# Hybrid encoder trunk on one core: rotary reads, output-weight loads, the MLP norm's mean and the half-piece mixes put in other places

## The chip, the cores and the metric

The kernel runs on one core of a Trainium2 chip. The metric is the device time of one execution in microseconds (us), the median of several runs; lower is better. Engines are named as the profile names them: PE (matrix products), DVE, ACT, POOL, SP (which only issues transfers here).

## The reference, cut to what matters

One sequence of 1024 tokens of width 1024 goes through two layers, all in float32. Layer 0 mixes tokens by grouped-query attention (16 heads of 64, 4 key heads), layer 1 by a chunked gMLP unit; each is followed by a squared-ReLU MLP of hidden width 4096. Every sub-layer is normed and modulated by a conditioning vector.

```python
q = apply_rope(rmsnorm(q, q_g), cos, sin)        # q and k of the attention
o = softmax(q @ k.T * HEAD_DIM ** -0.5) @ v ;  x += gate * (o @ w_o)
h = modulate(rmsnorm(x, g), shift, scale)        # before each mixer and each MLP
u, v = split(gelu(h @ w_in + b_in))              # gMLP
v = einsum('gpq,bnqgc->bnpgc', w_s, layernorm(v)) + b_s
x += gate * ((u * v) @ w_out)
x += gate * (square(relu(h @ w_in)) @ w_out)     # MLP
```

There are 16 position-mixing matrices of 128x128, each for a group of 192 of the 3072 gMLP channels.

## The kernel before, in words

Each large product is made in two levels. A float32 operand is split into a high and a low half (ACT copies the high half, a CAST; DVE or POOL subtracts for the low half), and three matmuls per pair of tiles take the place of one: lines L575 to L577 for q, k and v, L469 to L471 for the input products of gMLP and MLP, L1212 to L1214 for their output products. The input products are also cut into blocks that are combined by sums and differences (the "forms", t tiles), so that seven block products take the place of eight; `forms_b` builds the forms of the second half of the blocks from the normed x while PE already works on the first. The sub-layers follow each other: qkv, attention, the output weights wo, MLP 0, gMLP, MLP 1. A scheduler orders the instructions of each engine from the order of the program; on an engine, an instruction that waits holds up all behind it.

The places that the change and the prediction touch:

- qkv, about 100 to 130 us. `qk_sums` (L623) squares each q tile on ACT (L622) and sums it per head on DVE; `qk_rstd` adds the mean and takes the root (L641, L245 to L250); `qk_rope` applies the rotary tables: DVE multiplies the PSUM tile (L633, and L635 twice), POOL adds (L636); `qk_scale` (L649, POOL) multiplies by the root. For four q tiles (`ps`, named qkv_145 and qkv_146 in the order) squares, sums and roots come first, the rotary reads of PSUM behind them. The PSUM tiles are then taken by the next products (L575). `kstacks` (L681, PE transposes into PSUM tiles kt) needs tiles that DVE's L611 (`values`, low halves of v) has read.
- the end of attention, 455 to 505 us. The wo slabs come through `issue_w`: a transfer (L113, 512 KB), a CAST on ACT (L116), a subtraction on POOL (L117). Slots w (4 of them) are shared with the slabs that POOL scales for the conditioning (L199, L200). The x tiles (`load_x`, L520) are issued by SP ahead of the first two wo slabs. ACT also does what attention waits for: the exponentials (L957), the copies of PSUM tiles (L937, L968, L994, L996).
- the norm of each MLP. `norm_ss` sums squares on PE (L274), takes mean and epsilon on DVE (L276), a power on POOL (L242) and four scaled copies of the identity on ACT (L284); `norm_rb` broadcasts by a product (rb, L289), and `forms_b` starts with L334 on DVE. HB and HR count in which units of the input product the two calls stand.
- the mixes of the gMLP, 1507 to 1772 us. For each of 24 channel tiles of 128 and both halves of the tokens `mix` makes a product per 128 tokens (L1661) and DVE adds the bias (L1665); a channel tile with ct % 3 == 1 straddles two groups, so that its mix has two pieces of 64 channels: 8 tiles, 16 mixes of 16 matmul records with 64 columns of weights. The mixes stand between the products L469 to L471, spread by `at`.

Of the kernel before, what the change touches and what calls it, by code (L numbers as in the profile page):

```python
# [13 lines left out]
AF = mybir.ActivationFunctionType  # L14
ALU = mybir.AluOpType
# [4 lines left out]
D = 1024  # L20
# [16 lines left out]
def encoder_kernel(ctx: ExitStack, tc: tile.TileContext, t: dict, out: bass.AP):  # L37
# [18 lines left out]
    def hold(ins):  # L56
        if pinned[0]:
            pin(ins)
# [22 lines left out]
    def wide(tag, dt=F32, shape=(1024,)):  # L81
        if tag == "c":
            return cwide(dt, shape)
        return mem.tile([P] + list(shape), dt, tag=tag, name=nm(tag), bufs=SLOTS[tag])
# [17 lines left out]
    kw = (KT, P)  # L102
    plan = [(("wo", m), kw) for m in (*range(KT), *range(WA))]

    issued = []

    def issue_w():
        key, shape = plan[len(issued)]
        raw = wide("w", F32, shape)
        src = t[key[0]]  # L110
        for i in key[1:]:
            src = src[i]
        nc.sync.dma_start(raw, src)  # L113
        hi = wide("s", F32R, shape)
        lo = wide("s", F32R, shape)
        S.copy(hi, raw)  # L116
        G.tensor_tensor(lo, raw, f32(hi), ALU.subtract)  # L117
        issued.append((key, hi, lo))
# [148 lines left out]
    def norm_rstd(sqs, bank):  # L267
        return norm_rb(norm_ss(sqs, bank), bank)

    def norm_ss(sqs, bank, wide_dg=False):  # L270
        acc = sqs.acc
        ps = bank("ss")[:, :4]
        for j in range(4):
            hold(T.matmul(ps[:, j : j + 1], acc[:, j * P : (j + 1) * P], ones[:, 0:1], start=True, stop=True))  # L274
        ms = small.tile([P, 4], F32, tag="ms", name=nm("ms"))
        hold(V.tensor_scalar(ms, ps, 1.0 / D, EPS, ALU.mult, ALU.add))  # L276
        r = rsqrt_small(ms, 4)
        dg = slot()
        if wide_dg:
            hold(V.tensor_tensor(dg.rearrange("p (j q) -> p j q", j=4), ident.unsqueeze(1).broadcast_to([P, 4, P]),  # L280
                                 r.unsqueeze(2).broadcast_to([P, 4, P]), ALU.mult))
            return dg
        for j in range(4):
            S.activation(dg[:, j * P : (j + 1) * P], ident, AF.Copy, scale=r[:, j : j + 1])  # L284
        return dg
# [257 lines left out]
    if True:  # L543
# [100 lines left out]
        def q_sums(src):  # L644
            return qk_rstd(qk_sums(src))
# [177 lines left out]

        pk = banks(False)
        qkv_mm(0, 0, pk, hs1)
        rr2 = q_sums(ps)
        q_rope(0, 2, ps, rr2, (0, 1), G)
        qkv_mm(0, 1, pk, hs1)
        q_rope(0, 2, ps, rr2, (2, 3), G)
        qkv_mm(0, 2, pk, hs1)  # L830
        qkv_w(2, 0, V, True)
        kk = k_split(kd)
# [83 lines left out]
    with ExitStack() as es:  # L916
# [132 lines left out]
        for i in range(nu + 2):  # L1049
            u0 = units[i] if i < nu else None  # L1050
            u1 = units[i - 1] if 0 < i <= nu else None
            u2 = units[i - 2] if i > 1 else None
            if u0:
                if i % 4 == 0:
                    qst, nxt = nxt, []
                u0.qst = qst
            for op in ORDER.split():
                f, w, j = op[0], int(op[1]), int(op[2])
                if f == "m":
                    if i in deferred:  # L1060
                        deferred.pop(i)()
                    elif i == WO_AT - 6:
                        load_sel()
                    elif WO_AT <= i < WO_AT + 10:
                        if i == WO_AT:
                            copy_sel()
                        elif i == WO_AT + 1:
                            wo_sums(0)
                        else:
                            wo_prep(0, i - WO_AT - 2)  # L1070
                    elif i >= nu:
                        mods(1)
                    if late_mods and i % 4 == 1:
                        late_mods.pop()()
                    if i % 4 == 3 and 12 <= i < 52:
                        late_mods.append(mod_ahead())
                    slabs.step(bank_x, i >= 14 and (i % 4 in (1, 2) or i % 8 == 3))
                elif f == "q":
                    if i % 4 == 0 and w == 0 and i + 4 < nu:
                        qh = q_stage(units[i + 4].qq, units[i + 4].g)  # L1080
                    if i % 4 > 1 and w == 1 and i + 2 < nu:
                        q_trans(qh, i % 4 - 2, nxt)
                else:
                    u = (u0, u1, u2)[w]
                    if u and (i or f not in "se"):
                        stages[f](u, j)
            if i == nu - 1:
                x[0] = [load_x(0, k) for k in range(KT)]
            if i == nu:
                wo_mm(0, (0,), bank_x)  # L1090
# [249 lines left out]
    def mlp(layer, fs, sqs, done, hook):  # L1340
        hidden = forms_dram(16)
        out_ = Out(t["wm"][layer], hidden, 4, mod[:, layer, 5])
        quad = {}
        f = {}
        stores = []

        def sink(c, m, hf):
            S.activation(c, c, AF.Relu)
            S.activation(c, c, AF.Square)
            p = m // 2  # L1350
            quad[(m, hf)] = c
            q = early((m % 2, hf))
            if q:
                nc.scalar.dma_start(hidden[p][q], c)
                if q == "1" and p < FIRST:
                    del quad[(m, hf)]
                elif q == "2" and p < FIRST:
                    quad[(m - 1, 0)] = slot()
                    nc.sync.dma_start(quad[(m - 1, 0)], hidden[p]["1"])
            else:  # L1360
                tiles = {(j, h): quad.pop((m + j, h)) for j in range(2) for h in range(2)}
                stores.extend(spread(tiles, hidden[p], slot, V))

        n = 16 * 7
        rest = []
        halves = None if layer else Halves(late)

        def at(i):
            more(f, RW, None)
            if halves:  # L1370
                h = i - 13
                if 0 <= h < 2 * KT:
                    spill(h // KT, (h % KT,))
                elif h == 2 * KT:
                    halves.start()
                elif h == 2 * KT + 4:
                    halves.silu()
                    halves.load()
                    halves.load()
                elif h > 2 * KT + 6 and h % MX == 0:  # L1380
                    halves.step()
            if i == HB[layer]:
                rest.append(norm_ss(sqs[0], bank_y))
            elif i == HB[layer] + HR[layer]:
                rest[:] = forms_b(f, x[1], layer, 1, norm_rb(rest[0], bank_y, True), "5473")
            elif i > HB[layer] + HR[layer] and rest:
                rest.pop(0)()
            if stores and i % 7 > 0 and i % 7 != 6:
                stores.pop(0)()
            out_.ahead(i - n)  # L1390

        yield from winograd(lambda m: t["wi"][layer, m], 16, f, sink, FIRST, at, lambda: (cut(8), f.update(fs[0])))

        def at_out(i):
            if stores and i > 2:
                stores.pop(0)()
            if i == CUT:
                cut(4)
            if halves and i in XL:
                load_xs(*XL[i])  # L1400
            if hook and i >= out_.n - out_.tail:
                hook(i - out_.n + out_.tail)

        if halves:
            load_xs(*XL[-1])
        out_.run(at_out, done)
# [203 lines left out]
    def gmlp(f, sqB, done, hook):  # L1610
        rest = []

        def at(i):
            more(f, RW, None)
            if i == HBV:
                spill(0)
                rest.append(norm_ss(sqB, bank_y))
            elif i == HBV + 2:
                rest[:] = forms_b(f, x[1], 1, 0, norm_rb(rest[0], bank_y), "5734", True)
            elif rest and i in (*range(HBV + 3, HBV + 7), 10, 12, 16, 20):  # L1620
                rest.pop(0)()
                if len(rest) == 4:
                    spill(1)
# [65 lines left out]
        for p in range(12):  # L1689
            i = 7 * p  # L1690
            at(i - 4 if p else -1, load_v, p)
            for j in range(8):
                at(i - 1 + (j // 4) if p else -1, norm_v, p, j)
            if p % 3 == 0:
                at(i - 5 if p else -1, consts_load, p // 3)
                at(i if p else 3, consts, p // 3)
            for k, (j, hf) in enumerate(order):
                at(i + 2 + k + (0 if p else 2), mix, 2 * p + j, hf)
                at(i + ((3, 6, 6, 7)[k] if p else (6, 6, 7, 8)[k]), times, p, j, hf)
            at(i + (8 if p else 9), spread_uv, p)  # L1700
        steps.sort(key=lambda e: e[:2])

# [68 lines left out]
HK = 3  # L1771
LK = 4
HB = (2, 1)
HR = (2, 1)
HBV = 1
PRE = 2
WO_AT = 53
# [73 lines left out]
```

## Time and profile before

| | us |
|---|---|
| median of 3 runs (2625.09 to 2626.88) | 2625.38 |
| the profiled execution | 2627.54 |
| its span | 2625.8 |
| PE busy in it | 2601.6 (99%) |
| DVE busy | 2183.1 (83%) |
| ACT busy | 1451.1 (55%) |
| POOL busy | 723.2 (28%) |

The profiled execution took 2.2 us more than the median, and 1.7 us of it lie outside its span. A row of the timeline gives start, duration, engine, line of the program, operation, tiles and, in brackets, how long the engine had been idle before it and what released it. A matmul's duration is longer than its share of PE, since the next starts before it ends; PE's pace is read from starts.

### The profile page before, as it was taken

To read this page: it belongs to the slowest core of one execution; us is meant where nothing else is said; L and a number is where in the kernel's file an instruction comes from. 1 tells how busy PE (TensorE), PEld (TensorE's weight loads), DVE (VectorE), ACT (ScalarE), POOL (GpSimd) and SP (SyncE) were. 2 spreads that over 40 slices of the span, in tenths; PEclk is the share of its full clock that TensorE was granted. 3 is DMA by queue.
4 is the path that set the end of the run, shared out by engine and by line. 5 is a ranking of instruction groups with operands and counts; after the bars stand their busy time and mean duration, and the time that the engine had idled before them with its cause. 6 is when DMAs were issued, how large, how long until landed. Compare 5 with 4: busy or idle time off the path is not lost. (4 is left out here: it accounts for less than half of the span.)

```text
span 2625.8 us, 37307 instructions
## 1 busy us (share of the span) xinstructions
PE 2601.6 (99%) x12860; PEld 2172.2 (83%) x12860; DVE 2183.1 (83%) x3276; ACT 1451.1 (55%) x2612; POOL 723.2 (28%) x531
## 2 busy tenths in 40 slices
PE   9999999999999999999999999999999999999999
PEld 7789999888788888888888888888888788888887
DVE  7868999887989989877897687788979977789974
ACT  4569999854654455446543354445456645465442
POOL 0238776533000004430122054451520000005400
PEclk9999999999999999999999999999999999999999
DMA  8010222234486788545243355568641554487461
GB/s 306 27 33 9 74 88 75 97 112 145 168 288 245 270 310 306 192 133 172 82 136 121 120 174 175 178 204 305 237 141 50 177 179 156 153 310 268 149 211 58
DMA packets 208752, 435.39 MB, mean 166 GB/s; under 512 B 23025, under 2 KB 35441, under 8 KB 208562
## 3 DMA queue, kind: packets, MB, share of 16 engines
q1 hardware_dynamic: 181682, 395.24, 44.7%
q10 hardware_dynamic: 26880, 37.76, 4.0%
q8 instruction: 102, 1.67, 0.3%
q14 instruction: 88, 0.72, 0.1%
HBM read 310.23 MB, written 122.68 MB: 165 GB/s over the span
## 5 line engine op out<-in xcount | busy, mean ns | idle before, releaser
L1212 PE MATMUL out<-t,s 128*128 128x512 f32 x1232 | 479.9, 390 | 0.9 <-ACT t L328 0.8
L1213 PE MATMUL out<-t,s 128*128 128x512 f32 x1232 | 479.3, 389 | 0.7 <-DVE t L329 0.7
L1214 PE MATMUL out<-t,s 128*128 128x512 f32 x1232 | 478.9, 389 | 0.0
L469 PE MATMUL w<-t,s 128*128 128x512 f32 x1168 | 459.8, 395 | 0.9 <-ACT t L328 0.5
L470 PE MATMUL w<-t,s 128*128 128x512 f32 x1168 | 455.2, 390 | 1.8 <-DVE t L329 1.8
L471 PE MATMUL w<-t,s 128*128 128x512 f32 x1168 | 454.7, 389 | 0.0
L329 DVE TENSOR_TENSOR t<-t,t 128x512 fp32r<-128x512 f32 x408 | 324.7, 806 | 36.2 <-ACT t L328 29.0
L328 ACT CAST t<-t 128x512 fp32r<-128x512 f32 x408 | 245.3, 617 | 122.2 <-DMA t<-hf 71.7
L1213 PEld LDWEIGHTS out<-t,s 128*128 128x128 f32 x1232 | 231.2, 188 | 50.2 <-DVE t L329 1.8
L1212 PEld LDWEIGHTS out<-t,s 128*128 128x128 f32 x1232 | 231.2, 188 | 50.2 <-ACT t L328 1.7
L1214 PEld LDWEIGHTS out<-t,s 128*128 128x128 f32 x1232 | 231.2, 188 | 48.1
L454 ACT CAST s<-w 128x512 fp32r<-128x512 f32 x292 | 173.4, 616 | 161.4 <-PE w L471 104.3
L470 PEld LDWEIGHTS w<-t,s 128*128 128x128 f32 x1168 | 219.3, 188 | 49.7 <-DVE t L329 5.2
L469 PEld LDWEIGHTS w<-t,s 128*128 128x128 f32 x1168 | 219.3, 188 | 49.4 <-issue 2.9
L471 PEld LDWEIGHTS w<-t,s 128*128 128x128 f32 x1168 | 219.2, 188 | 45.6
L455 DVE TENSOR_TENSOR s<-w,s 128x512 fp32r<-128x512 f32 x292 | 221.8, 766 | 41.1 <-ACT s L454 40.6
L1194 ACT CAST s<-t 128x512 fp32r<-128x512 f32 x240 | 148.2, 620 | 187.0 <-PE out L1214 136.3
L1180 POOL TENSOR_TENSOR w<-w,t 128x512 f32<-128x512 f32 x20 | 34.2, 1721 | 767.7 <-DMA t<-hf 691.5
L1195 DVE TENSOR_TENSOR s<-t,s 128x512 fp32r<-128x512 f32 x240 | 195.1, 814 | 56.1 <-ACT s L1194 55.4
L951 DVE TENSOR_REDUCE mx<-s 128x1 f32<-128x1024 f32 x128 | 156.2, 1220 | 30.5 <-PE s L948 29.2
L974 DVE TENSOR_TENSOR t<-t,t 128x512 fp32r<-128x512 f32 x256 | 164.1, 681 | 17.1 <-ACT t L968 16.4
L984 PE MATMUL o<-t,t 128*128 128x256 f32 x1024 | 162.6, 291 | 0.0
(251 smaller groups left out, 5089.1 us busy)
## 6 DMA issues: line engine op xcount, KB each, us to landing
t<-hf SPq DMA_DIRECT2D x320, 256.0 KB, 4.0
hf<-c SPq DMA_DIRECT2D x156, 256.0 KB, 3.4
w<-in_wi_dram SPq DMA_DIRECT2D x64, 512.0 KB, 4.5
hf<-c ACTq DMA_DIRECT2D x96, 256.0 KB, 2.7
w<-in_ada_dram SPq DMA_DIRECT2D x36, 512.0 KB, 3.9
x<-in_ada_dram SPq DMA_DIRECT2D x64, 256.0 KB, 5.4
t<-in_wm_dram SPq DMA_DIRECT2D x64, 256.0 KB, 4.7
wf<-w SPq DMA_DIRECT2D x64, 256.0 KB, 3.0
```

The lines of the kernel that those rows point to most:

```text
L328: S.copy(hi, src)
L329: (eng or V).tensor_tensor(lo, src, f32(hi), ALU.subtract)
L454: S.copy(hi, src)
L455: V.tensor_tensor(lo, src, f32(hi), ALU.subtract)
L469: T.matmul(ps, hi[:, a], th, start=kt == 0, stop=False)
L470: T.matmul(ps, hi[:, a], tl, start=False, stop=False)
L471: T.matmul(ps, lo[:, a], th, start=False, stop=kt == 3)
L974: pin(V.tensor_tensor(lo, pt, f32(hi), ALU.subtract))
L1195: V.tensor_tensor(lo, src, f32(hi), ALU.subtract)
L1212: T.matmul(ps, hi[:, a], th, start=begin and kt == 0, stop=False, **g)
L1213: T.matmul(ps, hi[:, a], tl, start=False, stop=False, **g)
L1214: T.matmul(ps, lo[:, a], th, start=False, stop=end and kt == 3, **g)
```

## The change

1. In qkv the four rotary steps of that q set stand as `qk_rope`, two ahead of the sums of squares and two behind; the roots and the scalings are taken later.
2. `issue_w` is parted: `fetch_w` issues a slab's transfer, and two of them stand ahead of the x loads in attention's last unit.
3. `norm_ss` takes mean and epsilon by an ACTIVATE on ACT in both MLPs and in the gMLP's norm; in MLP 0 the broadcast product stands one unit earlier (HR 2 to 1); in both MLPs `forms_b` takes the differences for its forms "5" and "4" later (apart).
4. The two mixes of a straddling channel tile stand in the same unit, next to each other.

```diff
+    def fetch_w():
+        key, shape = plan[len(fetched)]
         raw = wide("w", F32, shape)
...
         nc.sync.dma_start(raw, src)
+        fetched.append(raw)
+
+    def issue_w():
+        key, shape = plan[len(issued)]
+        if len(fetched) == len(issued):
+            fetch_w()
+        raw = fetched[len(issued)]
...
+        if act:
+            S.activation(ms, ps, AF.Identity, scale=1.0 / D, bias=epst)
+        else:
+            hold(V.tensor_scalar(ms, ps, 1.0 / D, EPS, ALU.mult, ALU.add))
...
-        rr2 = q_sums(ps)
-        q_rope(0, 2, ps, rr2, (0, 1), G)
+        ds = [qk_rope(ps[j], 0, j, 1, V, G) for j in range(2)]
+        sums2 = qk_sums(ps)
+        ds += [qk_rope(ps[j], 0, j, 1, V, G) for j in range(2, 4)]
         qkv_mm(0, 1, pk, hs1)
-        q_rope(0, 2, ps, rr2, (2, 3), G)
+        rr2 = qk_rstd(sums2)
+        for j in range(4):
+            qk_scale(ds[j], rr2, j)
+            qn[(j, 1)] = ds[j]
...
             if i == nu - 1:
+                fetch_w()
+                fetch_w()
                 x[0] = [load_x(0, k) for k in range(KT)]
...
-                rest.append(norm_ss(sqs[0], bank_y))
+                rest.append(norm_ss(sqs[0], bank_y, act=True))
             elif i == HB[layer] + HR[layer]:
-                rest[:] = forms_b(f, x[1], layer, 1, norm_rb(rest[0], bank_y, True), "5473")
+                rest[:] = forms_b(f, x[1], layer, 1, norm_rb(rest[0], bank_y, True), "5473", True)
...
-                at(i + 2 + k + (0 if p else 2), mix, 2 * p + j, hf)
+                at(i + (4 if j in two else next(free)) + (0 if p else 2), mix, 2 * p + j, hf)
...
-HR = (2, 1)
+HR = (1, 1)
```

DVE in qkv. Tile qkv_145 holds the first two q tiles, qkv_146 the other two; qss are the sums, y, e and r the root. Before, the last reads of qkv_145 stand here:

```order
L633 TENSOR_TENSOR t_227_967<-qkv_145_658,t_141_638 128x512
L250 SCALAR_TENSOR_TENSOR r_212_909<-e_214_913,y_213_910 128x32
L641 TENSOR_SCALAR qss_219_945<-qss_219_945 128x32
L635 TENSOR_TENSOR t_228_968<-qkv_145_658,t_142_640 128x8x32
L246 RECIPROCAL y_225_960<-y_225_960 128x32
L635 TENSOR_TENSOR t_228_968<-qkv_145_658,t_142_640 128x8x32
L248 SCALAR_TENSOR_TENSOR e_226_963<-y_225_960 128x32
L633 TENSOR_TENSOR t_229_974<-qkv_145_658,t_141_638 128x512
L249 TENSOR_TENSOR e_226_963<-e_226_963,qss_219_945 128x32
L635 TENSOR_TENSOR t_230_975<-qkv_145_658,t_142_640 128x8x32
```

In the change they begin sixteen rows earlier, at the place of the first root:

```order
L652 TENSOR_SCALAR qss_201_865<-qss_201_865 128x16
L644 TENSOR_TENSOR t_219_945<-qkv_145_658,t_141_638 128x512
L254 RECIPROCAL y_205_874<-y_205_874 128x16
L646 TENSOR_TENSOR t_220_946<-qkv_145_658,t_142_640 128x8x32
L256 SCALAR_TENSOR_TENSOR e_206_877<-y_205_874 128x16
L646 TENSOR_TENSOR t_220_946<-qkv_145_658,t_142_640 128x8x32
L257 TENSOR_TENSOR e_206_877<-e_206_877,qss_201_865 128x16
L644 TENSOR_TENSOR t_221_951<-qkv_145_658,t_141_638 128x512
L258 SCALAR_TENSOR_TENSOR r_204_873<-e_206_877,y_205_874 128x16
```

L644, L646 and L652 are L633, L635 and L641 of before. Further on, one cast's low half (L577, L566 of before) that stood ahead of the reads for `kstacks` now stands behind them.

ACT at the end of attention. s are high halves of weight slabs, w the slabs. Before, the first wo slab's CAST stands in a late unit, between copies L968:

```order
L968 CAST t_1643_6318<-t_1642_6313 128x512
L116 CAST s_1841_7023<-w_1840_7021 128x1024
L968 CAST t_1646_6331<-t_1645_6326 128x512
L957 ACTIVATE c_1647_6333,rowsum_87<-s_1639_6304,mx_1640_6309 128x1024
L994 COPY t_1277_4968<-o_1632_6281 64x256
L996 COPY t_1649_6346<-o_1632_6281 64x256
L896 CAST t_1653_6358<-t_442_1903 128x512
L116 CAST s_1844_7029<-w_1843_7027 128x1024
```

In the change (lines L124, L983, L952, L972, L1009, L1011 are L116, L968, L937, L957, L994, L996 of before) both stand some six units earlier:

```order
L1011 COPY t_1510_5826<-o_1491_5754 64x256
L124 CAST s_1842_7025<-w_1817_6943 128x1024
L983 CAST t_1515_5848<-t_1514_5843 128x512
L952 CAST t_1517_5855<-qt_1516_5850 128x512
L983 CAST t_1520_5864<-t_1519_5859 128x512
L972 ACTIVATE c_1521_5866,rowsum_87<-s_1511_5831,mx_1512_5836 128x1024
L983 CAST t_1526_5882<-t_1525_5877 128x512
L983 CAST t_1529_5895<-t_1528_5890 128x512
L972 ACTIVATE c_1530_5897,rowsum_87<-s_1522_5868,mx_1523_5873 128x1024
L1009 COPY t_1140_4466<-o_1513_5838 64x256
L1011 COPY t_1532_5910<-o_1513_5838 64x256
L124 CAST s_1844_7029<-w_1818_6945 128x1024
```

The CAST stands right ahead of the copies of the unit in which the x loads are issued. On SP the order is now: first wo slab, two x tiles, second wo slab, six x tiles.

PE among the mixes (w and t are the products between them, x the operands of a mix). Before, the two mixes of the straddling tile 1 stand forty products apart, the first so:

```order
L471 MATMUL w6_3763_16191<-t_3361_13980,s_3753_16109 128x512
L1661 MATMUL mix_3764_16205<-x_3678_15717,x_3740_16046 64x128 x4
L1661 MATMUL mix_3764_16205<-x_3678_15717,x_3741_16048 64x128 x4
L469 MATMUL w5_3771_16228<-t_3367_14049,s_3755_16136 128x512
L470 MATMUL w5_3771_16228<-t_3368_14050,s_3755_16136 128x512
```

In the change (L1678 is L1661, L480 to L482 are L469 to L471):

```order
L482 MATMUL w4_3780_16258<-t_3425_14328,s_3758_16160 128x512
L1678 MATMUL mix_3781_16272<-x_3678_15717,x_3740_16046 64x128 x4
L1678 MATMUL mix_3781_16272<-x_3678_15717,x_3741_16048 64x128 x4
L1678 MATMUL mix_3783_16283<-x_3678_15717,x_3742_16050 64x128 x4
L1678 MATMUL mix_3783_16283<-x_3678_15717,x_3743_16052 64x128 x4
L480 MATMUL w7_3786_16298<-t_3385_14118,s_3762_16187 128x512
```

All eight pairs stand so, with nothing between them.

## Rows read from the trace of the kernel before

**Rows 1.** What PE waited for: releaser, total us, times, longest us.

```profile
PE w L470 <- DVE t L329: 1.8, 6, 0.5
PE w L469 <- ACT t L328: 1.7, 2, 1.2
```

**Rows 2.** PE in qkv, timeline 111 to 127 us.

```profile
113.59 0.47 PE L575 MATMUL qkv<-t,t 128*128 128x512 f32 x1 [2.11 <-DVE t L635]
...
115.05 0.60 PE L575 MATMUL qkv<-t,t 128*128 128x512 f32 x1
...
118.44 0.42 PE L576 MATMUL qkv<-t,t 128*128 128x512 f32 x1
...
126.31 0.89 PE L681 MATMUL kt<-identr,t 128*128 128x128 f32 x8
```

**Rows 3.** Stretches: us, busy PE, PEld, DVE, ACT, POOL, granted clock, DMA share, GB/s.

```profile
116.00:118.00 2.00, 2.00 (x6) 1.53 (x5) 2.00 (x2) 0.00 (x0) 2.00 (x2) 0.50 0.00 0
500.80:504.20 3.40, 3.40 (x14) 2.91 (x13) 1.39 (x3) 3.39 (x7) 3.40 (x7) 0.50 0.46 119
2044.40:2050.00 5.60, 5.17 (x22) 3.96 (x23) 5.60 (x11) 4.09 (x8) 0.00 (x0) 1.00 0.52 187
```

**Rows 4.** DVE in qkv, timeline 99 to 127 us.

```profile
103.35 0.25 DVE L246 RECIPROCAL y<-y 128x16 f32<-128x16 f32 x1 [1.60 <-ACT y L245]
...
117.14 1.76 DVE L566 TENSOR_TENSOR s<-c,s 128x512 fp32r<-128x512 f32 x1
...
124.04 0.68 DVE L672 TENSOR_TENSOR t<-t,t 128x512 fp32r<-128x512 f32 x1
...
125.84 1.41 DVE L611 TENSOR_TENSOR t<-qkv,t 128x256 fp32r<-128x256 f32 x4
```

**Rows 5.** ACT in qkv, timeline 105 to 113 us.

```profile
108.79 0.62 ACT L560 CAST w<-c 128x512 fp32r<-128x512 f32 x1 [1.24 <-PE qkv L577]
```

**Rows 6.** ACT at the end of attention, timelines 456 to 470 and 492 to 503 us.

```profile
460.46 0.37 ACT L996 COPY t<-o 64x256 f32<-64x256 f32 x1
...
461.35 0.59 ACT L937 CAST t<-qt 128x512 fp32r<-128x512 f32 x1
...
497.85 1.05 ACT L116 CAST s<-w 128x1024 fp32r<-128x1024 f32 x1 [2.27 <-DMA w<-in_wo_dram]
```

**Rows 7.** The same place on PE.

```profile
462.30 0.60 PE L965 MATMUL t<-ident,c 128*128 128x128 f32 x4
...
500.55 1.59 PE L965 MATMUL t<-ident,c 128*128 128x128 f32 x7 [1.89 <-ACT c L957]
```

**Rows 8.** POOL at 458 us, and the landing times of the wo slabs (L113, 14 of them).

```profile
458.36 2.40 POOL L200 TENSOR_TENSOR s<-s,w 128x1024 f32<-128x1024 f32 x1
...
DMA to landing us min/median/max: 3.2/3.7/8.8
```

**Rows 9.** The norm of MLP 0: ACT, DVE, POOL and PE, timelines 650 to 661 us.

```profile
653.57 0.59 ACT L474 COPY c<-w 128x512 f32<-128x512 f32 x1
656.79 1.28 ACT L284 ACTIVATE t<-ident,r 128x128 f32<-128x128 f32 x4 [2.62 <-POOL r L242]
...
658.61 0.69 DVE L329 TENSOR_TENSOR t<-t,t 128x512 fp32r<-128x512 f32 x1 [2.94 <-ACT t L328]
...
655.75 1.01 POOL L242 TENSOR_TENSOR r<-ms,mhalf 128x4 f32<-128x4 f32 x1 [19.06 <-DVE ms L276]
...
655.07 0.39 PE L469 MATMUL w<-t,t 128*128 128x512 f32 x1
```

**Rows 10.** PE around a straddling mix and around a whole one, timelines 1625 to 1632 us.

```profile
1629.62 0.39 PE L471 MATMUL w<-t,s 128*128 128x512 f32 x1
...
1631.30 0.40 PE L470 MATMUL w<-t,s 128*128 128x512 f32 x1
...
1625.99 0.39 PE L471 MATMUL w<-t,s 128*128 128x512 f32 x1
...
1627.34 0.40 PE L470 MATMUL w<-t,s 128*128 128x512 f32 x1
```

More of the change, by code (lines that the diff above doesn't have):

```diff
@@ L103, in encoder_kernel @@
     plan = [(("wo", m), kw) for m in (*range(KT), *range(WA))]
-    issued = []
-    def issue_w():
-        key, shape = plan[len(issued)]
+    issued, fetched = [], []
+    def fetch_w():
+        key, shape = plan[len(fetched)]
         raw = wide("w", F32, shape)
@@ L113, in issue_w @@
         nc.sync.dma_start(raw, src)
+        fetched.append(raw)
[4 more added lines that the diff above has]
+        raw = fetched[len(issued)]
+        fetched[len(issued)] = None
         hi = wide("s", F32R, shape)
@@ L268, in norm_rstd, with norm_ss @@
         return norm_rb(norm_ss(sqs, bank), bank)
-    def norm_ss(sqs, bank, wide_dg=False):
+    def norm_ss(sqs, bank, wide_dg=False, act=False):
         acc = sqs.acc
@@ L275, in norm_ss @@
         ms = small.tile([P, 4], F32, tag="ms", name=nm("ms"))
-        hold(V.tensor_scalar(ms, ps, 1.0 / D, EPS, ALU.mult, ALU.add))
+        if act:
+            S.activation(ms, ps, AF.Identity, scale=1.0 / D, bias=epst)
+        else:
+            hold(V.tensor_scalar(ms, ps, 1.0 / D, EPS, ALU.mult, ALU.add))
         r = rsqrt_small(ms, 4)
@@ L1616, in at @@
                 spill(0)
-                rest.append(norm_ss(sqB, bank_y))
+                rest.append(norm_ss(sqB, bank_y, act=True))
             elif i == HBV + 2:
@@ L1696, in gmlp @@
                 at(i if p else 3, consts, p // 3)
+            two = [j for j in range(2) if len(pieces[2 * p + j]) > 1]
+            free = iter((2, 3) if two else (2, 3, 4, 5))
             for k, (j, hf) in enumerate(order):
-                at(i + 2 + k + (0 if p else 2), mix, 2 * p + j, hf)
-                at(i + ((3, 6, 6, 7)[k] if p else (6, 6, 7, 8)[k]), times, p, j, hf)
+                at(i + (4 if j in two else next(free)) + (0 if p else 2), mix, 2 * p + j, hf)
+                at(i + ((5 if 0 in two else 3, 6, 6, 7)[k] if p else (7, 6, 7, 8)[k]), times, p, j, hf)
             at(i + (8 if p else 9), spread_uv, p)
```

## The prediction, made before the changed kernel was timed

> **What bounds the kernel now.** PE is busy for 99% of the span, so time goes only where PE stands still, runs at the lower clock, or spends longer on a product than it must. I read first what PE waited for, then the timelines around each long wait, then the granted clock behind it, and last the rows of PE itself where the mixes stand. Four places belong to the change.
>
> In qkv PE stood 2.11 us until DVE had made its last rotary read of a PSUM tile; 1.5 us after that restart matmuls begin to come slower, from 115.05 to 118.44, and the granted clock of that stretch is 0.50, the lower of the two levels, 1.2 GHz [rows 2, 3]. At half speed 3.4 us of work cost 1.7 more, so the place costs 2.11 + 1.7 = **3.8 us**. At the end of attention ACT stood 2.27 us for a wo slab [rows 6]; PE then stood 1.89 us [rows 7], and again 3.4 us follow at 0.50 [rows 3]: 1.89 + 1.7 = **3.6 us**. Behind the 1.2 us wait of MLP 1 [rows 1] the clock stays at 1.00 [rows 3]. So I price a pause of about 1.2 us at itself, and one of 1.9 us or more at itself plus 1.7. In MLP 0 PE loses 1.8 us in six small waits for DVE [rows 1], behind a stop of DVE of 2.94 us for the norm [rows 9]. In the gMLP the mixes wait for nothing to speak of: what the change touches there is PE's own work.
>
> **The change, part by part.** The profiled execution took 2627.54 us, 2.2 above the median of 2625.38; the terms are differences, which I put on the median. A measurement of this kernel tells about 0.2%, 5.25 us, from no change.
>
> *Rotary reads.* The order shows the reads of the first tile at the first root, where DVE was idle 1.60 us [rows 4]. They are done about 5 us earlier, so the wait of 2.11 goes, and with it the slow stretch: -3.8. But this brings PE to the transposes kt at 126.31 - 3.8 = 122.5, and these wait for DVE's L611, which started at 125.84 [rows 2, 4]. DVE's own way to that point is now the bound. It wins 1.45 of the idle 1.60 (a small operation still waits for the root) and 0.6 for the cast half that moves behind. It loses 1.2: the second root on ACT now stands behind a CAST that waits for PE until 108.79 and ends at 109.41 [rows 5], while DVE gets there at about 108.4. The third thing is POOL. A subtraction of this shape took 1.76 us beside POOL's work and 0.68 alone [rows 4], 1.1 us for each clash. Before, these and their like added some 4.5 us; in the new order POOL adds earlier and scales later, and I count two or three clashes, 2.8. So L611 starts at 125.84 - 1.45 - 0.6 + 1.2 - 1.7 = 123.3, its first read ends 0.4 later, and PE waits 123.7 - 122.5 = 1.2, short enough to keep the clock. Net **-2.6**. Ends: -3.8 if no clash is left, and +0.8 if all stay (wait 2.9, and the slow stretch of 1.7 behind it).
>
> *Loads of the wo slabs.* The transfer is now first on SP, but its slot comes free only when POOL has ended L200 at 458.36 + 2.40 = 460.76 [rows 8]. It lands 3.2 to 3.7 us later (fastest and median of 14) [rows 8], taken 3.3: 464.1. By the order its CAST stands right behind the copy L996 that began at 460.46 [rows 6], and so ACT, which ran without a gap here, stands about 3.2 us and then casts for 1.05 [rows 6]. Queued behind it on ACT are two copies, the second of which (L937) ended at 461.94, 1.1 us after L996 did; they now end at 464.1 + 1.0 + 1.0 = 466.1. PE's transposes, which started at 462.30 [rows 7], wait for these: **3.8 us**, and the slow stretch of 1.7. The second slab's slot waits for POOL's subtraction of the first; its CAST stops ACT again, for some 0.6 by the same walk. New cost 3.8 + 1.7 + 0.6 = 6.1, against the 3.6 that vanish near 500: net **+2.5**. Ends: -2.0 if the slab is there when ACT comes (then only the second's share and a short wait of 1 remain), +3.5 if it takes the median and a little more. The x loads that move behind it are not wanted before the wo products, 50 us and more later; I cost them at nothing, and a wait there of the size of a load, 3.7, if that cover were gone.
>
> On the clock, the rows show that the lower level began 1.5 us after the restart in one case and within 0.3 us in the other [rows 2, 3, 7]. The Trainium skill, "TensorE: Matmul & The Clock Gate", Part 1, says that the monitor's window runs freely and does not follow the kernel, so that the place of a drop depends on where in the window work falls. By that rule neither new pause need draw the slow stretch, and one of 1.2 us might; the two delays agree with it. With no slow stretch this part would be +0.8 in place of +2.5; that is a rival below.
>
> *The MLP norms.* In MLP 0 the mean was made on DVE, just before POOL's power at 655.75; ACT ends its copy at 653.57 + 0.59 = 654.2 and can do it there, the power (1.01) ends near 655.4 and the four copies (1.28) near 656.7, 1.4 earlier than before [rows 9]. The broadcast product, however, now stands where PE is at about 655.1 [rows 9], so PE waits 1.6 there. DVE, whose pace sets this stage, starts 1.4 earlier, and gives about 1.0 back when its first L477 waits for a product that is now later. Net **-0.5**; ends -1.8, all the small waits [rows 1], and +1.2, where the 1.6 draws the slow stretch. In MLP 1 the mean comes 0.25 earlier and the two sets of differences stand behind, which brings the first forms earlier by up to 1.2, two operations of 0.6; the wait was 1.2 [rows 1]. I take **-0.7**, between 0 and -1.2. In the gMLP's norm PE waited for nothing: 0, and the shift of 0.16 us of work from DVE to ACT is covered by ACT's idle time.
>
> *Mixes.* From a product before a mix to the second product behind it PE takes 1631.30 - 1629.62 = 1.68 us with a straddling mix and 1627.34 - 1625.99 = 1.35 with a whole one [rows 10]. The same number of columns goes in and out, so 0.33 is what going to the 64-column form and back costs. The order shows all 16 in 8 pairs with nothing between them: 8 x 0.33 = **-2.6**. Ends: 0, if the cost lies in each mix, and -2.6. The pair needs two PSUM tiles at once, of four; the whole mixes keep one or two, and DVE's additions have a whole unit.
>
> Sum: -2.6 + 2.5 - 0.5 - 0.7 - 2.6 = **-3.9**, 2625.38 - 3.9 = **2621.5 us**.
>
> **The rivals.**
> - *The slab is in time* (the wo part harmless): for it, an early start; against it, the POOL row, by which no slot is free before 460.76, and the order on ACT. Then that part is -2.0 to -3.6 in place of +2.5: 2625.38 - 3.9 - 4.5 to - 6.1, about 2616.
> - *No slow stretch at the new pause*: -3.9 - 1.7 = -5.6, 2619.8. For it the two different delays, against it that both pauses of 1.9 us and more were answered.
> - *The slab shares the engines with the x loads and lands late*, the one that ends above: among the 14 the slowest took 8.8 us [rows 8], behind x loads. If the first takes 8, ACT and PE wait 4.7 longer, +0.8 in all; if the second does too, up to 2631. It decides from a landing of 7.2 us (3.3 + 3.9). Against it: only two x tiles follow closely, on slots that free later than the slab's.
> - *The pauses only move*: all clashes stay on DVE, and the 1.6 at the MLP's norm draws the slow stretch: -3.9 + 3.4 + 1.7 = +1.2, 2626.6.
> - *Joining the mixes changes nothing*: -1.3, 2624.1.
>
> **How the numbers follow.** The forecast as summed 0.42; slab in time 0.15; no slow stretch 0.13; slab late 0.09; pauses moved 0.12; mixes alike 0.09. The range from 2615.5 to 2627.5 takes in all but the slab late and the tails. Faster by over 0.2% means below 2620.1: the first two rivals and a part of the forecast's own spread, 0.33. Slower means above 2630.6, the slab late and more: 0.07. Within 0.2%: 0.60.
>
> **What would show it.** In the changed profile: no wait at L575 near 113 and one of about 1.2 at kt; none at 500, and 3.8 near 462 behind ACT's wait for the first slab, with a granted clock of 0.50 behind it; the rb product waiting 1.6 in MLP 0; a pair of straddling mixes taking 2.1 us between its neighbours' starts, less than twice one. The forecast is wrong if the wait near 462 is under 1 or over 5 us, or if PE waits over 2 us at kt.

## The result and the profile after

The changed kernel takes 2629.49 us, median of 20 runs (2626.47 to 2634.09), against 2626.03 of the kernel before (20 runs, 2624.31 to 2629.42): a ratio of 1.0013, 95% interval 1.0007 to 1.0019, so 3.4 us or 0.13% slower. Forecast were 2621.5 us, with a range from 2615.5 to 2627.5. It lies within 0.2% of before, the case that had 0.60, but on the other side and outside the range.

The span of its profiled execution is 2628.2 us, 2.4 above before's 2625.8. What PE waited for, in part (releaser, total us, times, longest us):

```profile
PE t L980 <- ACT t L952: 4.1, 2, 3.8
PE rb L300 <- ACT t L295: 1.9, 1, 1.9
PE out L1229 <- DVE t L1281: 1.6, 2, 1.0
PE w L481 <- DVE t L340: 1.5, 3, 1.0
PE w L482 <- DVE t L340: 0.9, 1, 0.9
PE w L480 <- DVE c L1682: 0.8, 1, 0.8
PE kt L692 <- DVE t L622: 0.8, 1, 0.8
```

L980, L952, L300, L295, L692 and L622 are L965, L937, L289, L284, L681 and L611 of before; L481 and L482 are L470 and L471; L1229 is L1212, L340 is L329. L1281 is L1264, L1682 is L1665. The wait at L575 [rows 2] is gone, and a shorter one stands at kt, as forecast. The new first row is the wo slab's. On ACT it looks so (timeline; L1011, L124 and L983 are L996, L116 and L968 of before):

```profile
458.34 0.37 ACT L1011 COPY t<-o 64x256 f32<-64x256 f32 x1
462.06 1.04 ACT L124 CAST s<-w 128x1024 fp32r<-128x1024 f32 x1 [3.35 <-DMA w<-in_wo_dram]
463.01 0.58 ACT L983 CAST t<-t 128x512 fp32r<-128x512 f32 x1
463.48 0.59 ACT L952 CAST t<-qt 128x512 fp32r<-128x512 f32 x1
...
469.46 1.05 ACT L124 CAST s<-w 128x1024 fp32r<-128x1024 f32 x1
```

and on PE, with the granted clock of three stretches below it (columns as in [rows 3]):

```profile
124.36 1.86 PE L692 MATMUL kt<-identr,t 128*128 128x128 f32 x19 [0.76 <-DVE t L622]
...
464.13 1.10 PE L980 MATMUL t<-ident,c 128*128 128x128 f32 x4 [3.78 <-ACT t L952]
...
658.76 1.13 PE L300 MATMUL rb<-t,ones 128*128 128x512 f32 x2 [1.90 <-ACT t L295]
```

```profile
464.90:467.60 2.70, 2.70 (x15) 2.70 (x14) 1.83 (x4) 1.87 (x5) 2.70 (x2) 0.50 0.38 115
488.40:491.60 3.20, 3.20 (x16) 2.91 (x14) 3.20 (x2) 0.11 (x1) 2.78 (x2) 0.52 0.00 0
658.80:662.00 3.20, 3.20 (x12) 2.33 (x13) 2.08 (x4) 1.73 (x3) 0.00 (x0) 1.00 0.00 0
```

ACT stands 3.35 us for the slab, PE 3.78 for ACT, and the clock falls behind it. The second slab's CAST, at 469.46, waits for nothing. A second slow stretch (granted clock near 0.50, the 1.2 GHz level) at 488 follows no wait of that size, and the 1.90 at rb is followed by none. The joined mixes take what they should: from the product before a pair to the second behind it

```profile
1653.24 0.39 PE L482 MATMUL w<-t,s 128*128 128x512 f32 x1
1653.56 1.97 PE L1678 MATMUL mix<-x,x 128*64 128x128 f32 x32
1655.45 0.50 PE L480 MATMUL w<-t,s 128*128 128x512 f32 x1
1655.79 0.40 PE L481 MATMUL w<-t,s 128*128 128x512 f32 x1
```

2.55 us pass, 2.10 without the two products of 0.227; a single straddling mix took 1.68 - 0.45 = 1.23 [rows 10]. A pair saves 0.36, eight 2.9.

**Where the time went.** I matched each PE product with its twin in the trace of before and took the difference of their starts, in us, at places of the program (times of before). The difference between two columns is what a kernel won or lost between them. The last column but one is the end of the gMLP; the first is not the change's, since nothing there differs and kernels scatter from -0.8 to +1.5. A profile is one execution and can lie some us off its kernel's median, so the table tells where time went, and the medians and ratios what a part is worth. The rows belong to the experiments below: "late CASTs" means that the two CASTs of the wo slabs stand later on ACT, "HR 2" that the broadcast product of MLP 0 keeps its old unit.

| kernel | 19 | 126 | 455 | 645 | 701 | 1506 | 1776 | 2007 | 2066 |
|---|---|---|---|---|---|---|---|---|---|
| the change | 1.4 | -2.0 | -2.1 | 1.7 | 2.2 | 3.8 | 1.3 | 3.2 | 2.4 |
| the change, second profile | 1.3 | -1.6 | -1.8 | 0.1 | 2.4 | 3.9 | 1.9 | 3.1 | 2.3 |
| rotary reads alone | 0.8 | -2.2 | -2.1 | -1.9 | -1.8 | -1.0 | -1.9 | -3.2 | -3.2 |
| fetch alone | -0.5 | -0.7 | -0.6 | 4.6 | 4.6 | 5.5 | 4.6 | 3.6 | 3.6 |
| norms alone | -0.5 | -0.2 | -0.1 | -1.4 | 0.8 | 1.6 | 1.0 | -0.4 | -1.1 |
| norms alone, HR 2 | -0.6 | -1.1 | -1.2 | -0.5 | -0.9 | -0.2 | 0.0 | -0.7 | -1.4 |
| mixes alone | 1.5 | 1.5 | 1.5 | 1.0 | 1.0 | 1.0 | 0.0 | 2.1 | 3.7 |
| change, late CASTs | 1.3 | -1.7 | -1.8 | -4.4 | -3.8 | -2.2 | -3.6 | 0.5 | -0.4 |
| late CASTs, HR 2, no mixes | -0.8 | -4.2 | -4.2 | -7.8 | -8.3 | -7.7 | -8.3 | -8.9 | -9.5 |
| late CASTs, HR 2, all parts | -0.6 | -3.2 | -3.3 | -4.9 | -5.2 | -4.5 | -8.3 | -7.6 | -8.5 |

### The profile page after: what moved, and what is told of

Its sections match the earlier page's. It is cut to its first block, busy times and chain, and to the rows that moved or that the text cites. A ratio compares the mean times of both kernels' runs of the same rounds, so it can differ in the third digit from the quotient of the medians.

```text
span 2628.2 us, 37319 instructions
## 1 busy us (share of the span) xinstructions
PE 2602.0 (99%) x12860; PEld 2176.4 (83%) x12860; DVE 2185.5 (83%) x3273; ACT 1450.3 (55%) x2615; POOL 724.4 (28%) x531
## 4 chain that ended last, share of the span: by engine, by line
PE 56%; DMA 1%; DVE 1%; ACT 0%; issue 0%; POOL 0%; SPq 0%; DVEq 0%; ACTq 0%
PE out L1229 9%; PE out L1231 9%; PE out L1230 9%; PE w L480 6%; PE w L482 6%; PE w L481 6%; PE v L1586 3%; PE v L1588 3%; PE v L1587 3%; PE mix L1678 2%; DVE t L340 0%; DMA x<-vd 0%; DMA w<-in_wi_dram 0%; DMA t<-wf 0%; DMA t<-hf 0%
## 5 line engine op out<-in xcount | busy, mean ns | idle before, releaser
L1229 PE MATMUL out<-t,s 128*128 128x512 f32 x1232 | 480.7, 391 | 3.0 <-DVE t L1281 1.6
L480 PE MATMUL w<-t,s 128*128 128x512 f32 x1168 | 459.6, 394 | 0.8 <-DVE c L1682 0.8
L481 PE MATMUL w<-t,s 128*128 128x512 f32 x1168 | 454.9, 390 | 1.5 <-DVE t L340 1.5
L482 PE MATMUL w<-t,s 128*128 128x512 f32 x1168 | 455.0, 390 | 0.0
L340 DVE TENSOR_TENSOR t<-t,t 128x512 fp32r<-128x512 f32 x408 | 332.3, 825 | 30.6 <-ACT t L339 23.1
L1229 PEld LDWEIGHTS out<-t,s 128*128 128x128 f32 x1232 | 231.3, 188 | 53.3 <-ACT t L339 2.7
L481 PEld LDWEIGHTS w<-t,s 128*128 128x128 f32 x1168 | 219.5, 188 | 48.9 <-DVE t L340 3.9
L466 DVE TENSOR_TENSOR s<-w,s 128x512 fp32r<-128x512 f32 x292 | 216.4, 748 | 51.6 <-ACT s L465 50.6
L480 PEld LDWEIGHTS w<-t,s 128*128 128x128 f32 x1168 | 219.5, 188 | 47.9 <-issue 1.7
L482 PEld LDWEIGHTS w<-t,s 128*128 128x128 f32 x1168 | 219.4, 188 | 45.2
L1212 DVE TENSOR_TENSOR s<-t,s 128x512 fp32r<-128x512 f32 x240 | 194.4, 811 | 56.4 <-ACT s L1211 55.8
L989 DVE TENSOR_TENSOR t<-t,t 128x512 fp32r<-128x512 f32 x256 | 164.3, 683 | 19.3 <-ACT t L983 18.4
```

The lines of the kernel that those rows point to most:

```text
L340: (eng or V).tensor_tensor(lo, src, f32(hi), ALU.subtract)
L466: V.tensor_tensor(lo, src, f32(hi), ALU.subtract)
L480: T.matmul(ps, hi[:, a], th, start=kt == 0, stop=False)
L481: T.matmul(ps, hi[:, a], tl, start=False, stop=False)
L482: T.matmul(ps, lo[:, a], th, start=False, stop=kt == 3)
L989: pin(V.tensor_tensor(lo, pt, f32(hi), ALU.subtract))
```

## The experiments

Theory A, from the two traces: the rotary reads and the mixes bring what was forecast; the fetch loses more than forecast because its CAST stands too early on ACT, and the norm part loses in MLP 0 because its broadcast product stands a unit early. The rivals are named in each expectation. Each ratio is to the kernel before on the same chip; its interval of 0.0009 either way is 2.3 us. The edits are cut to the lines that tell them.

**The change without the fetch.**

```diff
             if i == nu - 1:
-                fetch_w()
-                fetch_w()
                 x[0] = [load_x(0, k) for k in range(KT)]
```

> The change without its second part (the wo loads stay behind the x loads). Theory A, by the two traces: the fetch costs about 3.3 us at its own place (462 to 505 us), and the norm part makes the new small pauses in MLP 0 and its output stage (+2.1). Then this kernel is 3.3 us faster than the change, at or about 1 to 2 us below the kernel before, and the waits near 690, 1067 and 1236 us stay. Rival B: the fetch also reshuffles the later stages; then it is some 5 to 6 us faster than the change, about 4 us below before, and those waits are gone.

2626.51 us, ratio 0.9998 (0.9989 to 1.0006): level with before, and about 3.9 below the change by the ratios, where Theory A said 3.3. The waits at rb (1.9) and near 690 (1.1) stayed and that at 1236 too, as Theory A had it; that at 1067 went, as Rival B had it. The price of the fetch fits Theory A; the 1 to 2 us below before that it gave the rest is not seen, though the interval allows it.

**Rotary reads and mixes alone.** Against before:

```diff
-        rr2 = q_sums(ps)
-        q_rope(0, 2, ps, rr2, (0, 1), G)
+        ds = [qk_rope(ps[j], 0, j, 1, V, G) for j in range(2)]
...
+                at(i + (4 if j in two else next(free)) + (0 if p else 2), mix, 2 * p + j, hf)
```

> The kernel before with the rotary reads and the joined mixes alone. Theory A: -2.8 from the rotary reads (wait at kt under 1.2 us, clock kept) and -2.0 to -2.6 from the mixes, so 4.8 to 5.4 us below before, no new wait in MLP 0. Rival C: the joined mixes reorder DVE in the gMLP's output stage, where the change shows 1.7 us of new waits (1864 to 1880 us); then only about 3.1 below before. Rival D: the gains of both parts are eaten by waits behind them; within 1 us of before.

The same edit moves the whole mixes and the multiplications behind the mixes (`times`, on POOL, the last on DVE) to other units, so what follows is the worth of the whole part, not of the joining alone.

2622.35 us, 0.9987 (0.9978 to 0.9996): 3.4 us won by the ratio, near Rival C's 3.1, though the interval holds Theory A's 4.8 as well. In the profile the mixes' stage gave 2.6 us, and a wait of 1.45 stood at 1868 in the gMLP's output stage, against 0.79 in before.

**The norm part alone.** Against before:

```diff
+                rest.append(norm_ss(sqs[0], bank_y, act=True))
...
-HR = (2, 1)
+HR = (1, 1)
```

> The kernel before with the norm part alone. Theory A: the rb product one unit earlier waits 1.6 to 1.9 us, MLP 0's norm stage ends 0.8 us later and its output stage adds 1.2, MLP 1 gains 0.7: 1 to 1.5 us above before. Rival B: these losses came with the fetch; then 0.5 to 1.2 below before as forecast.

2627.45 us, 1.0006 (0.9997 to 1.0015). The time is not told from before, but the trace is plain: rb waits 1.9, the clock behind it is low,

```profile
PE rb L292 <- ACT t L287: 1.9, 1, 1.9
```

```profile
656.30:659.60 3.30, 3.30 (x9) 2.40 (x8) 2.59 (x5) 1.86 (x3) 0.00 (x0) 0.54 0.00 0
```

and MLP 0's norm ends 2.2 us later (table, 645 to 701). MLP 1 gains 0.8. By the trace Rival B falls: the loss in MLP 0 is there without the fetch.

**The fetch alone.** Against before:

```diff
             if i == nu - 1:
+                fetch_w()
+                fetch_w()
```

> The kernel before with the early fetch of two wo slabs alone. Theory A: ACT stops about 3.3 us for the first slab, PE 3.8 us near 462 with the slow stretch of 1.5 to 1.7 behind it, against the 3.5 us that go near 500: 1.8 to 2 us above before, 3.3 if a second slow stretch comes near 488 as in the change's trace. Rival B: 4.5 or more above before, with new waits in the output stage of MLP 0 (1067, 1236 us).

2629.96 us, 1.0012 (1.0003 to 1.0021), so 3.2 us lost. The wait near 465 was 3.95 us, and two slow stretches stand behind it, the first twice as long as elsewhere (the rows lie within them):

```profile
465.80:471.60 5.80, 5.77 (x24) 5.48 (x25) 3.33 (x5) 4.90 (x10) 4.09 (x3) 0.50 0.50 180
492.00:495.60 3.60, 3.60 (x19) 3.31 (x18) 3.08 (x3) 2.13 (x4) 2.02 (x2) 0.53 0.00 0
```

In the output stage of MLP 0 one wait of 0.9 stood at 1238, none at 1067. Theory A, at its upper price.

**The transfer early, the CAST late.** Against the change, and the decisive one for this part: on SP the wo slabs and x tiles stand as in the change (the slabs issued at 459.0 and 465.2 us, there at 458.7 and 465.6), and the place of the two CASTs on ACT differs, which `pin` keeps in program order.

```diff
-            if i == nu - 1:
-                fetch_w()
-                fetch_w()
+            if i == 53:
+                fetch_w()
+                fetch_w()
+            if i in (56, 58):
+                issue_w(True)
...
+        cp = S.copy(hi, raw)
+        if fix:
+            pin(cp)
```

> The change, with the transfers of the two wo slabs issued at the same place on SP, but their CASTs on ACT kept in program order some 7 and 10 units later (near 503 and 523 us). Theory A (the cost is the place of the CAST on ACT, not the transfer): no wait near 462, no slow stretch behind it nor near 488, each CAST costs PE at most 0.5 us: 4 to 5 us faster than the change, 0.5 to 1.5 below before. Rival E (the early transfers themselves disturb the x loads or the slabs of POOL): the gain is under 2 us and new waits for DMA or POOL show between 465 and 560 us.

2621.85 us, 0.9986 (0.9978 to 0.9995): 6 to 7 us below the change's two measurements by the ratios, more than expected. The CASTs came at 496.77 and 509.68, behind data that had long landed; PE waited 0.24 us behind the second and nothing behind the first, and from 20 us to 2624 no stretch of the run had a low clock. ACT and PE in that kernel:

```profile
496.77 1.05 ACT L124 CAST s<-w 128x1024 fp32r<-128x1024 f32 x1
...
509.68 1.05 ACT L124 CAST s<-w 128x1024 fp32r<-128x1024 f32 x1
...
511.74 0.66 PE L982 MATMUL t<-ident,c 128*128 128x128 f32 x4 [0.24 <-ACT t L954]
```

So the fetch's loss was the order on ACT, not the transfer: Rival E falls. The profiled execution, 2627.11, was the longest of this kernel's eleven: its row of the table gains 2.6 between 455 and 645, and loses 4.1 in the gMLP's output stage, more than any other.

**Rotary reads, mixes and late CASTs.** Against the kernel above:

```diff
-                rest.append(norm_ss(sqs[0], bank_y, act=True))
+                rest.append(norm_ss(sqs[0], bank_y))
...
-HR = (1, 1)
+HR = (2, 1)
```

> Rotary reads, joined mixes and the early wo transfers with late CASTs; the norm part left out. Theory A: as the kernel with rotary reads and mixes alone (-3.8 measured), less the 1.7 to 2.4 us that PE waits near 500 there, plus at most 0.5 for the CASTs: 5.5 to 6 us below before. Rival E: no better than -3.8.

2621.47 us, 0.9983 (0.9974 to 0.9992): 4.5 us won, 1 us beyond the kernel without the early loads by the ratios, between Theory A's 5.5 and Rival E's 3.8, and the noise holds both. In the profile the gain between 455 and 645 is 3.4, where the kernel without the early loads has 0.2.

**The norm part with the broadcast product in its old unit.** Against the norm part alone:

```diff
-HR = (1, 1)
+HR = (2, 1)
```

> The norm part alone, but with the broadcast product of MLP 0 left in its old unit (HR 2). Theory A (the loss in MLP 0 is the earlier unit): the rb wait of 1.9 us and the slow stretch behind it are gone, rb waits for nothing, MLP 0 gains 0.2 to 0.7 and MLP 1 keeps its 0.75: 1 to 1.5 us below before. Rival F (the loss comes from the differences taken later): MLP 0 still ends 0.8 us or more later, and the wait of 1.0 us near 690 stays; 0 to 0.5 above before.

2624.22 us, 0.9997 (0.9988 to 1.0006). rb waits for nothing, and the six small waits that follow [rows 1] are all left (L473 and L332 are L470 and L329 of before):

```profile
PE w L473 <- DVE t L332: 1.7, 6, 0.4
```

MLP 0's norm ends 0.4 earlier instead of 2.2 later, MLP 1 gains 0.6: Theory A in the trace, by which Rival F falls; the ratio can't tell 1 us.

**All parts, both mended.** Against the kernel with the late CASTs:

```diff
-HR = (1, 1)
+HR = (2, 1)
```

> All four parts, with late CASTs of the wo slabs and the broadcast product in its old unit. Theory A: -2.8 (rotary reads), -2 (wo), -1 (norms), -2.5 (mixes), plus 0.5 to 1 for waits that the new orders of DVE bring in the output stages: 7 to 8 us below before. Rival G (parts take from one another): no better than the kernel without the norm part.

2619.69 us, 0.9973 (0.9963 to 0.9982): 7.1 us below before, as Theory A had it, and 2.6 beyond the kernel without the norm part. That speaks against Rival G; the two intervals overlap.

**The mixes alone.** Against before:

```diff
+                at(i + (4 if j in two else next(free)) + (0 if p else 2), mix, 2 * p + j, hf)
```

> The kernel before with the joined mixes alone. Theory A: 2.5 us gained between 1507 and 1775 us, 0.31 for each of 8 pairs, and 0.7 to 1.5 given back in the gMLP's output stage (waits of PE for DVE near 1860 to 1880 us beyond the 0.8 of before), since the joined order ends with another order of DVE: 1 to 1.8 us below before. Rival H (those waits come from elsewhere): nothing given back, 2.5 below.

2628.24 us, 1.0006 (0.9997 to 1.0014), and neither theory had it: no gain. The trace shows two places. In the mixes' own stage a wait of 1.39 us for DVE's addition cut the gain to 1.0 (table, 1506 to 1776); and the gMLP's output stage lost 2.1 us, where kernels without joined mixes win 0.5 to 1.4 on the profile of before. The waits:

```profile
PE out L1212 <- DVE t L1264: 1.6, 2, 1.0
PE out L1212 <- ACT s L1194: 0.7, 1, 0.7
PE w L469 <- DVE c L1665: 1.6, 2, 1.4
```

In the output stage of before PE waits so:

```profile
PE out L1212 <- ACT t L328: 0.8, 1, 0.8
```

L1264 is DVE's addition of an output product. The first of them stands on DVE in before and in this kernel at

```profile
1858.51 0.68 DVE L1264 TENSOR_TENSOR t<-out,t 128x512 f32<-128x512 f32 x1
```

```profile
1862.20 0.68 DVE L1264 TENSOR_TENSOR t<-out,t 128x512 f32<-128x512 f32 x1
```

while the first output product starts at 1774.9 in both. DVE comes 3.7 us later to the work that PE waits for. From that product to that addition 82.0 to 84.0 us pass in the six profiles with parted mixes, and 86.1 to 89.4 in the nine with joined ones. Behind MLP 1's wait of 1.2 a slow stretch came on top, which cost 1.6.

**The rotary reads alone.** Against before:

```diff
+        ds = [qk_rope(ps[j], 0, j, 1, V, G) for j in range(2)]
+        sums2 = qk_sums(ps)
+        ds += [qk_rope(ps[j], 0, j, 1, V, G) for j in range(2, 4)]
```

> The kernel before with the rotary reads alone. Theory A: PE's wait of 2.1 us at 113 and the slow stretch behind it go, a wait of 0.7 to 0.8 appears at kt, and the lead of 2.8 us at kt is kept to the end: 2.5 to 3 us below before in the profile, less in the median if the slow stretch at 115 doesn't come in all executions of the kernel before: then 1.3 to 2. Rival D: the lead is eaten by attention; within 0.5 of before.

2623.18 us, 0.9984 (0.9975 to 0.9993): 4.2 us won by the ratio, more than Theory A's 2.5 to 3, within the noise. The lead at kt, 2.9 us since 19, was kept to the end, as Theory A had it.

**The change once more.** No edit.

> The change once more, for a second profile. Theory A: the wait of 3.8 us near 462 is there again, with a slow stretch behind it; the second slow stretch near 488 and the one behind the rb product (658 us) may come or not. Rival J (the second slow stretch belongs to the stop of ACT): it is there again. 3 to 4 us above before.

2629.42 us, 1.0010 (1.0001 to 1.0019), so 2.6 us lost, in place of 3 to 4. The wait near 464 was 3.78 again, the slow stretch behind it there; that near 488 was not, and one behind rb was. Rival J falls.

**The mixes' worth, both sides on one chip.** All parts mended, without the joined mixes and, again, with them; the first against the second:

```diff
-                at(i + (4 if j in two else next(free)) + (0 if p else 2), mix, 2 * p + j, hf)
+                at(i + 2 + k + (0 if p else 2), mix, 2 * p + j, hf)
```

> All parts but the joined mixes, with late CASTs of the wo slabs and the broadcast product in its old unit. Theory K (the mixes give back what they win, by DVE's order in the gMLP's output stage): PE's waits between 1860 and 1885 us are under 0.9 us, the mixes' stage takes 2.5 us more, and the median is within 1.5 us of the kernel with the mixes joined. Theory A as forecast (the mixes are worth 2.6 us): 2.5 us or more slower than that kernel.

> The kernel with all four parts, late CASTs and the old unit for the broadcast product once more, beside the one without joined mixes on the same chip: 6 to 8 us below before. Theory K: within 1.5 us of the kernel without joined mixes; theory A: 2.5 or more faster.

2619.58 us without, 0.9978 (0.9969 to 0.9987), and 2619.49 with, 0.9975 (0.9966 to 0.9984). Theory K: the mixes' part brought nothing that can be measured, 0.1 us by the medians and 0.8 by the ratios. The waits of the output products, without and then with (those for ACT's L341 stand in MLP 0's output stage, near 1225):

```profile
PE out L1235 <- DVE t L342: 0.7, 1, 0.7
PE out L1234 <- ACT t L341: 0.6, 1, 0.6
PE out L1234 <- DVE t L1286: 0.5, 1, 0.5
```

```profile
PE out L1234 <- DVE t L1286: 1.0, 1, 1.0
PE out L1234 <- ACT t L341: 0.8, 1, 0.8
PE out L1235 <- DVE t L342: 0.7, 1, 0.7
PE out L1234 <- ACT s L1216: 0.6, 1, 0.6
```

In the two profiles the stage of the mixes won 3.9 us with and 0.7 without; of the 3.2 between them the output stage took 1.3 back. The 1.9 left are not in the medians. The execution with them was longer for another reason, a slow stretch near 482, so the profiles don't settle it. Both of these kernels, 6.5 and 6.6 us below before by their medians, beat both kernels of the case.

## Why the prediction was wrong, by its own steps

The forecast was -3.9 and the result +3.4. All the signs that the prediction named came out, and neither of the two by which it would be wrong: no wait at L575, 0.76 at kt, 3.78 near 462 with a slow stretch behind it, none at 500, 1.9 at rb, 2.10 for a pair. The waits that it looked for were right; what failed is what it costed at nothing around them. By their ratios the four parts alone come to -4.2 + 3.2 + 1.6 + 1.6 = +2.2, against +3.4 and +2.6 for the change: within the noise the parts add up, and against the terms of the sum (-2.6, +2.5, -1.2, -2.6) the mixes are off by 4.2 and the norms by 2.8.

**The rotary reads, -2.6: right in its sign and path, its size in part by luck.** The trace of the change gains 3.4 between 19 and 126, the part alone 2.9 and 4.2 in its ratio. The wait at kt was 0.76, where 1.2 was worked out, and the clock was kept. Inside the sum the roots went otherwise: 1.45 of DVE's idle 1.60 was to go and 1.2 to come back, and DVE stood 1.00 and 0.66, nothing won in all:

```profile
104.31 0.25 DVE L254 RECIPROCAL y<-y 128x16 f32<-128x16 f32 x1 [1.00 <-ACT y L253]
...
110.53 0.35 DVE L254 RECIPROCAL y<-y 128x32 f32<-128x32 f32 x1 [0.66 <-ACT y L253]
```

So the other two terms, the moved half and the clashes with POOL, must have brought more than the 2.3 that they were given.

**The wo slabs, +2.5: the mechanism right, the size too small.** "It lands 3.2 to 3.7 us later" and the wait of "3.8 us, and the slow stretch of 1.7" came as said: ACT 3.35, PE 3.78 and, in the second profile, 3.78 again. The 0.6 for the second slab did not come. Two terms failed. The 3.6 us "that vanish near 500" vanished, but they were those of one execution of before: in the six other kernels with the old loads PE waited 0.9 to 2.0 us there, and a slow stretch followed in one of the six profiles (HR 2). And with the new stop a second slow stretch stood in two of three profiles, and a first one of twice the length in one of these. The part alone cost 3.2 by its ratio, and 1.9 to 5.2 us between 455 and 645 in the three profiles.

**The norm of MLP 0, -0.5: wrong in its sign.** The wait at rb was sized well, 1.9 against 1.6. That DVE "starts 1.4 earlier" was to pay for it; DVE's first form came 1.0 earlier, and of the 1.8 us of small waits 1.5 stayed (L481, three in place of six). So from 645 to 701 the change lost 0.5, and its second profile 2.3, since there the 1.9 drew the slow stretch, as it did in three of the five profiles with this wait. That was the upper end of this term, +1.2, passed by 1 us. With the product in its old unit the same part gained 0.4. MLP 1's -0.7 was right: 0.6 to 1.0 in all kernels with the part.

**The mixes, -2.6: right in their own stage, wrong as a term.** This term failed by most. PE's own saving was 0.36 for each pair. "DVE's additions have a whole unit" put the wait for them at nothing; PE waited 0.3 to 1.6 us in that stage for DVE's additions in seven of nine profiles with joined mixes (and 0.3 and 0.8 in two of the six without). And nothing was costed for what comes behind: in the next stage, 1776 to 2007, where DVE comes later to its additions, all nine lost 0.6 to 4.1 us against before (the mixes alone 2.1), and all five others won 0.5 to 1.4. PE stood 2.2 to 3.9 us in that stage with joined mixes and 0.7 to 1.5 without. In all, the part was worth +1.6 us alone, +0.8 on top of the rotary reads and -0.8 on top of everything else, by the ratios, in place of -2.6. Whether the joining itself shifts DVE's work, or the units to which the edit moves the whole mixes and the multiplications, was not tried. The rival that gave the mixes nothing was named at 0.09, for another reason.

**What was not costed at all.** The output stage of MLP 0 lost 1.5 us in both profiles of the change (701 to 1506), at two places. Near 1067, where PE waits for DVE, the five profiles with rb a unit early lost 0.2 to 1.0 us and the other nine under 0.1, so this goes with the norm part's earlier product. Near 1236, behind a transfer's end, twelve of the fourteen profiles lost 0.3 to 1.0, the rotary reads alone among them; only the mixes alone and the rotary reads with the mixes did not. What this one hangs on is not shown.

Put together for the pair of profiles: +1.4 before the change begins, -3.4, -0.1, +3.8, +0.5, +1.6, -2.5, +1.9, -0.8, in the order of the columns: +2.4. The first of these is scatter.

## What to carry to other kernels

A transfer that is issued earlier can cost time if what consumes it moves forward as well: look up where the consumer now stands in its engine's order, and whether the data can be there by then. Here holding the consumer back, with the same early transfer, was worth 6 to 7 us against the change. A saving on the busiest engine need not be a saving of time where the next stage waits for another engine whose order the same edit shuffles; cost the order behind the edit too. And signs that all come true do not make a sum right: ask of each term at nothing what would show it. A price read off one execution should be read off two, where a clock's fall is part of it.

## What the runs showed of the clock

In the fifteen profiles, from 100 us on, a stretch at 1.2 GHz came with all three pauses of PE of 3.8 to 3.95 us, all five of 2.1 us (in qkv), five of the eight of 1.9 to 2.0, and one of the ten of 1.2 to 1.6. At the same place of the same program it came and did not: behind the 1.9 us at rb in the second profile of the change, not in the first. The pause of 1.2 us in MLP 1, which the forecast held too short, drew one in the profile of the mixes alone. The forecast priced every pause of the longer kind at 1.7 more, and the shorter at nothing. The Trainium skill, "TensorE: Matmul & The Clock Gate", Part 1, says that the monitor's window runs free of the kernel. The two outcomes at rb fit that; the 2.1 us in qkv were answered in all five profiles, as priced.

A slow stretch also came with no wait of note ahead of it (the longest of the 20 us before was 0.33), in the kernel with the rotary reads alone:

```profile
480.43 1.95 PE L209 MATMUL am<-ones,s 128*128 128x1 f32 x16
482.24 1.98 PE L952 MATMUL s<-x,t 128*128 128x512 f32 x4
```

```profile
480.00:482.00 2.00, 1.89 (x19) 1.71 (x18) 0.98 (x2) 1.96 (x5) 0.05 (x1) 1.00 0.00 0
482.60:485.40 2.80, 2.80 (x11) 2.43 (x11) 1.30 (x2) 0.00 (x0) 0.07 (x1) 0.50 0.00 0
```

Ahead of it stand sixteen products of a single column that took 1.95 us. The same happened at this place in four of the fifteen profiles, the one at 488 of the change among them, and in none behind the same sixteen products near 336 and 406. What draws it is not shown.
